# Differential output gates in the gate stage, four merge gates raw beside the attention, weight sums in two wide blocks, decay transposes later

## The chip, the core and the metric

The kernel runs on one core of one Trainium2 chip. TensorE (PE in the rows) multiplies, VectorE (DVE), ScalarE (ACT) and GpSimd (POOL) work elementwise, SyncE (SP) and ScalarE issue the transfers. The metric is the device time of one execution in microseconds. All inputs are float32, a batch of one, 1024 tokens, width 1024.

## What is computed

Two layers of a decoder trunk. Each reads one wide projection of the normalised input three ways (forgetting attention, "f"; differential attention, "d"; a gated short convolution), and merges the three branches with sigmoid gates:

```python
def _layer(x, ...):
    h = _rmsnorm(x, pre_g)
    p = h @ w_in
    (fq, fk, fv, ff, fg, dq, dk, dv, dg, cb, cc, cx, cg, mg) = _split_cols(p)
    log_f = jax.nn.log_sigmoid(ff + b_f)
    y_fox = _fox_attention(fq, fk, fv, log_f) * jax.nn.silu(fg)
    y_diff = _diff_attention(rotary(dq), rotary(dk), dv, lam, lam_init, diff_g) * jax.nn.silu(dg)
    y_conv = cb * _short_conv(cc * cx, conv_w) * jax.nn.silu(cg)
    gates = jax.nn.sigmoid(mg + b_m).reshape(b, s, N_BRANCH, D_MODEL)
    m = gates[:, :, 0] * (y_fox @ w_fox) + gates[:, :, 1] * (y_diff @ w_diff) + gates[:, :, 2] * (y_conv @ w_conv)
    return x + _rmsnorm(m @ w_o, post_g)
```

Inside the forgetting attention the decay c is the running sum of log_f over the tokens.

## The kernel before, in words

**Products in three parts.** Every float32 operand is split into a high part (a cast) and a low part (the operand less the high part). mm3 (lines 353 to 355) multiplies low by high, high by low and high by high. One matmul covers 128 rows, 128 weight columns and 512 tokens.

**Strassen pairs.** Most of the projection runs as pairs of two chunks of 128 columns: emit_pair loads the two weight chunks fa and fb (1024 columns each, two halves u and d) and makes four weight tiles from them, x = fa, y (its halves are the sums t2 and t3), z (its halves are t1 and t4) and b (one half of fb). put makes the high part on ScalarE (line 320) and the low part on GpSimd (line 321); the sums are VectorE subtractions (line 323). A pair is then seven products of 12 matmuls. Tiles for high and low parts have three buffers for the four tiles of a pair, so a tile is made while the pair before is still multiplied. The sums t1, t2 and t3 stand in a pool with two buffers (swaps). Each layer has 20 pairs: six for the convolution's and four for its merge gates, four for the differential q and k, and six for output gates and merge gates (gates_spilled), two ahead of the merge pairs and four between and behind the q and k pairs. The rope of q and k has one multiply per step on GpSimd (line 753), the convolution adds on GpSimd (line 561).

**Forget.** After the pairs, forget makes log_f on VectorE and ScalarE in small steps (lines 679 to 692), stops, and then transposes it on TensorE (line 701) and scans it on VectorE (line 703). Between the two parts the layer steps a projection (qk, "f", 2) four times.

**Attention.** Eight windows follow, four of forgetting heads and four of differential heads. In each window other work is interleaved with the attention's own: PLAN lists it. An entry qk or v is a projection, mg and dg a gate chunk that is computed plainly and stored raw, without its activation (24 matmuls of 512 columns for each of two token halves), y is the product of the attention's output and its output gate, split in two parts (y_prep), and br is one merge of the forgetting branch (merge_br: 24 matmuls of 512 columns). Where a gate was stored raw, y_prep runs a sigmoid on ScalarE (line 1124) and one more multiply on VectorE (line 1121), and merge_br runs a sigmoid of 1024 columns (line 1147). In the attention, line 988 is the exponential of the differential heads, lines 871 and 872 split the transposed probabilities, lines 1029 to 1031 multiply them by v, and lines 1044 and 1045 are the logarithm and exponential by which a head's output is normalised. ScalarE has to load a table (ACT_TABLE_LOAD) when it goes from one group of functions to another.

**Behind the attention** come the merges that PLAN does not name, the eight of the differential branch, and the output projection.

**What sets the order.** Each engine runs its instructions in one order. All engines but SyncE are ordered by a scheduler ahead of time, from the program's order and its own costs; SyncE's instructions stand as written. The pool blocks (41 buffers of 128 x 1024) serves the large intermediate tiles in turn. The kernel's layer function makes the gate pairs from all chunks of mg, fg and dg that PLAN does not name, in that order.

Of the kernel before, what the change touches and what calls it, by code (L numbers as in the profile page):

```python
# [11 lines left out]
F32 = mybir.dt.float32  # L12
# [10 lines left out]
P = 128  # L23
# [25 lines left out]
)  # L49
FILLS = {f for w in PLAN for f in w}  # L50
COST = {"v": 20.8, "qk": 20.8, "dg": 10.4, "mg": 10.4, "load": 0.0, "y": 1.0, "br": 5.2}
# [85 lines left out]
class Trunk:  # L137
# [168 lines left out]
    def emit_pair(self, l, i0, i1):  # L306

        nc = self.nc  # L310
        fa, fb = (self.ws.tile([P, 1056], F32, tag="wraw", name=self.nm("wraw"))[:, :1024] for _ in range(2))
        nc.sync.dma_start(fa, self.io["wt"][l, i0])
        nc.sync.dma_start(fb, self.io["wt"][l, i1])
        u, d = slice(0, 512), slice(512, 1024)

        def new():
            return [self.ws.tile([P, 1056], F32R, tag=t, name=self.nm(t))[:, :1024] for t in ("whi", "wlo")]

        def put(w, o, f):
            nc.scalar.copy(w[0][:, o], f)  # L320
            nc.gpsimd.tensor_tensor(out=w[1][:, o], in0=f, in1=w[0][:, o].bitcast(F32), op=ALU.subtract)  # L321

        sub = lambda o, a, b: nc.vector.tensor_tensor(out=o, in0=a, in1=b, op=ALU.subtract)  # L323
        x = new()
        put(x, slice(0, 1024), fa)
        t1, t2 = self.sw(), self.sw()
        sub(t1, fb[:, u], fa[:, u])
        sub(t2, fb[:, d], t1)
        y = new()
        put(y, u, t2)  # L330
        z = new()
        put(z, u, t1)
        t3 = self.sw()
        sub(t3, fb[:, d], fb[:, u])
        sub(t2, fa[:, d], t2)
        put(y, d, t3)
        put(z, d, t2)
        b = new()
        put(b, u, fb[:, d])
        r = lambda t: t.rearrange("p (k c) -> p k c", c=128)  # L340
        x, y, z, b = [[r(t) for t in o] for o in (x, y, z, b)]
        lo4, hi4 = (lambda p: [t[:, :4] for t in p]), (lambda p: [t[:, 4:] for t in p])
        return dict(b11=lo4(x), b21=hi4(x), t2=lo4(y), t3=hi4(y), t1=lo4(z), t4=hi4(z), b22=lo4(b))
# [867 lines left out]
    def layer(self, l):  # L1211
# [42 lines left out]
        decay = self.forget(L)  # L1254
        next(decay)
        first = self.qk_unit(L, "f", 2)
        for _ in range(4):
            next(first)
        run(decay)
        run(first)  # L1260
# [3 lines left out]
        for n, spec in enumerate(PLAN):  # L1264
# [6 lines left out]
            for f in spec:  # L1271
# [8 lines left out]
                elif f[0] == "load":  # L1280
                    gens.append(self.load_head(L, f[1]))
                    f = ("qk", "d", f[1])
# [136 lines left out]
```

## Time and profile before

| | us |
|---|---|
| median of three runs (2508.68 to 2515.22) | 2514.5 |
| profiled execution | 2515.5 |
| its span in the trace | 2513.7 |
| TensorE busy | 2406.0 (96%) |
| VectorE busy | 1539.6 (61%) |
| ScalarE busy | 1120.4 (45%) |
| GpSimd busy | 865.3 (34%) |

Layer 0 runs from 0 to about 1290 us, layer 1 from there to the end. In layer 0 the pairs run to about 560, the attention from 594 to 1107, the merges to 1175. The profiled execution is 1.8 us longer than its span and lies within the runs shown. In the views, a wait is idle time of an engine, put down to the instruction that released it.

### The profile page before, as it was taken

How to read it: one execution, taken by the hardware profiler on the slowest of the kernel's cores; microseconds unless marked ns; L12 is line 12 of the kernel's file. 1: busy time of each engine (PE TensorE's matmuls, PEld its weight loads, DVE VectorE, ACT ScalarE, POOL GpSimd, SP SyncE). 2: the span in 40 equal slices, each digit the busy share in tenths (PEclk: the TensorE clock that was granted, in tenths of full speed). 3: DMA queues.
4: the chain of work that ended last, by engine and by line, in shares of the span. 5: the costliest groups of instructions: out<-in, count | busy, mean ns of one | idle time of the engine just before them, and what ended most of it. 6: DMA issues, size and time to landing. Idle time of an engine off the chain costs nothing. (4 is left out here: it accounts for less than half of the span.)

```text
span 2513.7 us, 35377 instructions
## 1 busy us (share of the span) xinstructions
PE 2406.0 (96%) x12984; PEld 2037.3 (81%) x12984; DVE 1539.6 (61%) x2785; ACT 1120.4 (45%) x2294; POOL 865.3 (34%) x693
## 2 busy tenths in 40 slices
PE   6899999999999999989989999999999999999898
PEld 5677887787899888768967778887889898887688
DVE  4866466645665666667477664356465656667654
ACT  4323334335555545564453232233355655445542
POOL 0657325442222202451026663254322221125500
PEclk9999999999999999999999999999999999999999
DMA  4112234441223333644431122344422233346434
GB/s 162 42 51 72 98 99 140 155 164 53 77 70 118 110 101 114 198 154 151 151 142 43 51 92 84 105 136 146 151 64 74 75 94 108 105 139 212 148 110 184
DMA packets 117948, 285.54 MB, mean 114 GB/s; under 512 B 15616, under 2 KB 36480, under 8 KB 117776
## 3 DMA queue, kind: packets, MB, share of 16 engines
q1 hardware_dynamic: 67568, 212.69, 25.0%
q10 hardware_dynamic: 50208, 70.60, 9.1%
q8 instruction: 103, 1.69, 0.3%
q14 instruction: 69, 0.57, 0.1%
HBM read 196.06 MB, written 68.29 MB: 105 GB/s over the span
## 5 line engine op out<-in xcount | busy, mean ns | idle before, releaser
L281 POOL TENSOR_TENSOR wlo<-wraw,whi 128x1024 fp32r<-128x1024 f32 (+2 forms) x93 | 196.3, 2113 | 609.4 <-ACT whi L278 542.2
L353 PE MATMUL F<-ht,wlo 128*128 128x512 f32 x792 | 329.1, 416 | 0.0
L355 PE MATMUL F<-ht,whi 128*128 128x512 f32 x792 | 314.5, 397 | 0.0
L354 PE MATMUL F<-ht,whi 128*128 128x512 f32 x792 | 314.0, 396 | 0.2 <-DVE ht L375 0.2
L321 POOL TENSOR_TENSOR wlo<-sw,whi 128x512 fp32r<-128x512 f32 x160 | 226.2, 1424 | 218.9 <-ACT whi L320 193.2
L321 POOL TENSOR_TENSOR wlo<-wraw,whi 128x1024 fp32r<-128x1024 f32 x80 | 158.3, 1981 | 174.1 <-ACT whi L320 165.0
L320 ACT CAST whi<-sw 128x512 fp32r<-128x512 f32 x160 | 96.3, 619 | 245.6 <-DVE sw L323 97.3
L988 ACT ACTIVATE p<-S,sm 128x512 f32<-128x512 f32 (+2 forms) x192 | 110.5, 579 | 152.4 <-DVE sm L984 60.2
L355 PEld LDWEIGHTS F<-ht,whi 128*128 128x128 f32 x792 | 149.7, 189 | 33.3
L872 DVE TENSOR_TENSOR pt<-T,pt 128x512 fp32r<-128x512 f32 (+1 forms) x240 | 148.4, 633 | 42.1 <-ACT pt L871 40.1
L937 POOL TENSOR_TENSOR cB<-cB,tri 128x128 f32<-128x128 f32 x128 | 58.5, 462 | 328.6 <-DVE sm L898 276.8
L354 PEld LDWEIGHTS F<-ht,whi 128*128 128x128 f32 x792 | 150.9, 191 | 25.0 <-DVE ht L375 0.9
L353 PEld LDWEIGHTS F<-ht,wlo 128*128 128x128 f32 x792 | 150.6, 190 | 25.1 <-ACT ht L374 0.4
L278 ACT CAST whi<-wraw 128x1024 fp32r<-128x1024 f32 (+2 forms) x126 | 117.8, 940 | 84.1 <-PE F L355 22.5
L871 ACT CAST pt<-T 128x512 fp32r<-128x512 f32 (+1 forms) x240 | 124.4, 544 | 47.2 <-PE T L176 35.6
L833 PE MATMUL S<-qk,qk 128*128 128x512 f32 (+2 forms) x384 | 136.9, 357 | 5.3 <-ACT p L988 5.1
L982 DVE TENSOR_REDUCE sm<-S 128x1 f32<-128x512 f32 (+2 forms) x192 | 102.4, 552 | 54.4 <-PE S L837 27.8
L176 PE MATMUL T<-ident,p 128*128 128x128 f32 x864 | 127.6, 274 | 6.2 <-DVE p L999 4.7
L320 ACT CAST whi<-wraw 128x1024 fp32r<-128x1024 f32 x80 | 66.7, 834 | 140.8 <-PE S L355 43.8
L834 PE MATMUL S<-qk,sw 128*128 128x512 f32 (+2 forms) x384 | 129.3, 343 | 0.0
L905 ACT ACTIVATE p<-p,sm 128x1024 f32<-128x1024 f32 (+7 forms) x128 | 99.6, 779 | 50.8 <-DVE sm L898 38.9
L353 PE MATMUL F<-whi,ht 128*128 128x256 f32 (+1 forms) x416 | 121.0, 291 | 0.0
(379 smaller groups left out, 7060.2 us busy)
## 6 DMA issues: line engine op xcount, KB each, us to landing
wraw<-wt SPq DMA_DIRECT2D x128, 512.0 KB
mg<-tmp ACTq DMA_DIRECT2D x64, 256.0 KB
sw<-qk ACTq DMA_DIRECT2D x256, 64.0 KB
g<-mg SPq DMA_DIRECT2D x32, 512.0 KB
wraw<-wo SPq DMA_DIRECT2D x32, 512.0 KB
x<-x SPq DMA_DIRECT2D x24, 512.0 KB
wraw<-wbr SPq DMA_DIRECT2D x48, 256.0 KB
m<-tmp ACTq DMA_DIRECT2D x32, 256.0 KB
```

The source lines that it names most:

```text
L176: self.nc.tensor.transpose(out, x, self.ident)
L278: nc.scalar.copy(hi, raw)
L281: getattr(nc, eng).tensor_tensor(out=lo, in0=raw, in1=hi.bitcast(F32), op=ALU.subtract)
L320: nc.scalar.copy(w[0][:, o], f)
L321: nc.gpsimd.tensor_tensor(out=w[1][:, o], in0=f, in1=w[0][:, o].bitcast(F32), op=ALU.subtract)
L353: nc.tensor.matmul(ps, wl, xh, start=start and i == 0, stop=False)
L354: nc.tensor.matmul(ps, wh, xl, start=False, stop=False)
L355: nc.tensor.matmul(ps, wh, xh, start=False, stop=stop and i == n - 1)
L833: nc.tensor.matmul(ps[:, :wp], q[:, i * P:(i + 1) * P], k[:, c0:c0 + wp], start=True, stop=False)
L834: nc.tensor.matmul(ps[:, :wp], qsw[:, (i % 2) * P:(i % 2) * P + P], k[:, c0:c0 + wp], start=False, stop=not (last and guard))
L871: self.clock.later(0.1, lambda: nc.scalar.copy(hi, T[:, n0:]))
L872: done = self.clock.later(0.6, lambda: nc.vector.tensor_tensor(out=lo, in0=T[:, n0:], in1=hi.bitcast(F32), op=ALU.subtract))
```

## The change

PLAN no longer names the differential output gates dg 0 to 3; it names the merge gates mg 4 to 7 in the same windows, raw. So the gate pairs of a layer, until now mg 0 to 7 and fg 0 to 3, become mg 0 to 3, fg 0 to 3 and dg 0 to 3: six as before. The y steps of the differential heads then read finished gates, and merges 4 to 7 of the forgetting branch read raw ones. Merge 4 leaves the last window and runs behind the attention. In emit_pair the sums t1 to t3 leave the two swap buffers; two whole blocks sy and sz take all four sums, and y and z are cast and subtracted once each over 1024 columns. The projection in front of the decay's second part is stepped seven times in place of four.

```diff
@@ -42,10 +42,10 @@
     (("qk", "f", 0), ("v", "f", 0)),
     (("qk", "f", 1),),
     (("mg", 8), ("load", 0), ("v", "d", 0), ("mg", 9)),
-    (("mg", 10), ("load", 1), ("mg", 11), ("dg", 0)),
+    (("mg", 10), ("load", 1), ("mg", 11), ("mg", 4)),
     (("mg", 12), ("load", 2), ("v", "d", 1), ("mg", 13)),
-    (("mg", 14), ("load", 3), ("mg", 15), ("y", "f", 0), ("dg", 2), ("y", "f", 1), ("dg", 1), ("y", "f", 2), ("y", "f", 3)),
-    (("dg", 3), ("br", 0), ("br", 1), ("y", "d", 0), ("br", 2), ("y", "d", 1), ("br", 3), ("br", 4), ("y", "d", 2)),
+    (("mg", 14), ("load", 3), ("mg", 15), ("y", "f", 0), ("mg", 5), ("y", "f", 1), ("mg", 6), ("y", "f", 2), ("y", "f", 3)),
+    (("mg", 7), ("br", 0), ("br", 1), ("y", "d", 0), ("br", 2), ("y", "d", 1), ("br", 3), ("y", "d", 2)),
 )
@@ -321,20 +321,15 @@
         sub = lambda o, a, b: nc.vector.tensor_tensor(out=o, in0=a, in1=b, op=ALU.subtract)
-        x = new()
+        x, y, z = new(), new(), new()
         put(x, slice(0, 1024), fa)
-        t1, t2 = self.sw(), self.sw()
-        sub(t1, fb[:, u], fa[:, u])
-        sub(t2, fb[:, d], t1)
-        y = new()
-        put(y, u, t2)
-        z = new()
-        put(z, u, t1)
-        t3 = self.sw()
-        sub(t3, fb[:, d], fb[:, u])
-        sub(t2, fa[:, d], t2)
-        put(y, d, t3)
-        put(z, d, t2)
+        sy, sz = (self.blk([P, 1024], F32, "st") for _ in range(2))
+        sub(sz[:, u], fb[:, u], fa[:, u])
+        sub(sy[:, u], fb[:, d], sz[:, u])
+        sub(sy[:, d], fb[:, d], fb[:, u])
+        sub(sz[:, d], fa[:, d], sy[:, u])
+        put(y, slice(0, 1024), sy)
+        put(z, slice(0, 1024), sz)
         b = new()
         put(b, u, fb[:, d])
@@ -1254,7 +1249,7 @@
         first = self.qk_unit(L, "f", 2)
-        for _ in range(4):
+        for _ in range(7):
             next(first)
         run(decay)
```

Lines behind emit_pair move up by five. Three places in the engines' orders, each before and after.

GpSimd, at the first pair with a rope step, in layer 0. wlo is a low part, wraw a loaded weight, sw and st sums, tmp a q or k tile; before:

```order
L321 TENSOR_TENSOR wlo_2519<-wraw_2492,whi_2518 128x512
L753 TENSOR_TENSOR tmp_2786<-tmp_2786,rope_2717 128x512
L321 TENSOR_TENSOR wlo_2728<-wraw_2723,whi_2727 128x1024
L321 TENSOR_TENSOR wlo_2736<-sw_2732,whi_2735 128x512
L321 TENSOR_TENSOR wlo_2740<-sw_2731,whi_2739 128x512
L321 TENSOR_TENSOR wlo_2740<-sw_2732,whi_2739 128x512
L753 TENSOR_TENSOR tmp_2851<-tmp_2851,rope_2718 128x512
L321 TENSOR_TENSOR wlo_2736<-sw_2743,whi_2735 128x512
L321 TENSOR_TENSOR wlo_2751<-wraw_2724,whi_2750 128x512
```

and after:

```order
L321 TENSOR_TENSOR wlo_2454<-wraw_2432,whi_2453 128x512
L748 TENSOR_TENSOR tmp_2716<-tmp_2716,rope_2652 128x512
L321 TENSOR_TENSOR wlo_2663<-wraw_2658,whi_2662 128x1024
L321 TENSOR_TENSOR wlo_2665<-st_2670,whi_2664 128x1024
L321 TENSOR_TENSOR wlo_2667<-st_2671,whi_2666 128x1024
L748 TENSOR_TENSOR tmp_2781<-tmp_2781,rope_2653 128x512
L321 TENSOR_TENSOR wlo_2681<-wraw_2659,whi_2680 128x512
```

The second half of y (wlo_2736 from sw_2743) stood behind both halves of z and the rope step; now y is whole ahead of z, and the rope step stands behind z.

TensorE, at the decay of layer 0. F is the projection that stands around it, S takes the transposes (L701 before, L696 after); before:

```order
L355 MATMUL F_4278<-ht_107,whi_3958 128x512
L353 MATMUL F_4278<-ht_107,wlo_3959 128x512
L701 MATMUL S_4265<-ident,tmp_4206 8x128 x4
L701 MATMUL S_4271<-ident,tmp_4206 8x128 x4
L354 MATMUL F_4278<-ht_108,whi_3958 128x512
L355 MATMUL F_4278<-ht_107,whi_3958 128x512
```

and after:

```order
L348 MATMUL F_4178<-ht_107,wlo_3875 128x512
L349 MATMUL F_4178<-ht_108,whi_3874 128x512
L350 MATMUL F_4178<-ht_107,whi_3874 128x512
L348 MATMUL F_4178<-ht_110,wlo_3875 128x512
L349 MATMUL F_4178<-ht_111,whi_3874 128x512
L350 MATMUL F_4178<-ht_110,whi_3874 128x512
L348 MATMUL F_4178<-ht_113,wlo_3875 128x512
L349 MATMUL F_4178<-ht_114,whi_3874 128x512
L350 MATMUL F_4178<-ht_113,whi_3874 128x512
L696 MATMUL S_4204<-ident,tmp_4122 8x128 x4
L696 MATMUL S_4210<-ident,tmp_4122 8x128 x4
```

Before, four matmuls of that F bank's projection stood ahead of the transposes; now 18 do, 14 more (the rows show nine of the 18).

ScalarE, at the end of layer 0's last window. O is an attention output, od its copy, g a gate; before:

```order
L1040 ACTIVATE tmp_10118<-O_9945 128x256
L1041 COPY od_9645<-O_9945 128x256
L871 CAST pt_10120<-T_10121 128x384
L1044 ACT_TABLE_LOAD
L1044 ACTIVATE tmp_10118<-O_9945,eps 128x256
L1045 ACT_TABLE_LOAD
L1045 ACTIVATE tmp_10118<-tmp_10118 128x256
L1040 ACTIVATE tmp_10137<-O_10119 128x256
L1041 COPY od_9645<-O_10119 128x256
L1044 ACT_TABLE_LOAD
L1044 ACTIVATE tmp_10137<-O_10119,eps 128x256
L1045 ACT_TABLE_LOAD
```

and after:

```order
L1035 ACTIVATE tmp_9980<-O_9842 128x256
L1036 COPY od_9555<-O_9842 128x256
L866 CAST pt_9982<-T_9983 128x384
L1121 CAST yd_9935<-od_8031 128x512
L1039 ACTIVATE tmp_9980<-O_9842,eps 128x256
L1040 ACTIVATE tmp_9980<-tmp_9980 128x256
L1035 ACTIVATE tmp_10001<-O_9981 128x256
L1036 COPY od_9555<-O_9981 128x256
L1039 ACTIVATE tmp_10001<-O_9981,eps 128x256
```

Of eleven table loads at the end of each layer's attention one is left, ahead of the first sigmoid of the merges behind it.

## Rows read from the trace of the kernel before

**Rows 1.** TensorE's waits, whole program: engine, tile, line, releaser: us, times, longest

```profile
PE S L353 <- POOL wlo L321: 14.1, 4, 8.2
...
PE F L353 <- POOL wlo L321: 9.8, 3, 3.7
...
PE S L701 <- DVE tmp L692: 5.8, 2, 2.9
```

**Rows 2.** Stretches: length, busy time and instructions of each engine, granted clock, DMA share, GB/s

```profile
95.20:105.50 10.30, 5.52 (x13) 4.35 (x14) 9.97 (x10) 1.62 (x3) 4.87 (x4) 0.50 0.15 51
...
573.10:576.50 3.40, 3.40 (x9) 2.64 (x8) 3.25 (x4) 0.59 (x1) 0.00 (x0) 0.50 0.00 0
...
1467.40:1474.20 6.80, 5.96 (x14) 4.71 (x15) 3.01 (x5) 2.58 (x4) 4.32 (x3) 0.50 0.10 39
```

**Rows 3.** Groups by form: line, engine, tile, shape, count, busy us, mean ns, idle before

```profile
L321 POOL TENSOR_TENSOR wlo<-sw,whi 128x512 fp32r<-128x512 f32 x160 | 226.2, 1424 | 218.9 <-ACT whi L320 193.2 <-DVE tmp L527 25.6
...
L321 POOL TENSOR_TENSOR wlo<-wraw,whi 128x1024 fp32r<-128x1024 f32 x40 | 98.2, 2454 | 130.3 <-ACT whi L320 130.3
...
L320 ACT CAST whi<-sw 128x512 fp32r<-128x512 f32 x160 | 96.3, 619 | 245.6 <-DVE sw L323 97.3 <-PE S L355 44.9 <-PE T L355 28.2
...
L320 ACT CAST whi<-wraw 128x1024 fp32r<-128x1024 f32 x40 | 42.0, 1049 | 117.1 <-PE S L355 35.8 <-issue 22.7 <-PE F L355 21.1
```

**Rows 4.** Timeline of a pair that keeps pace: start, us, instruction, idle before, releaser

```profile
150.82 1.28 POOL L321 TENSOR_TENSOR wlo<-sw,whi 128x512 fp32r<-128x512 f32 x1 [2.73 <-ACT whi L320]
...
153.66 2.54 POOL L321 TENSOR_TENSOR wlo<-sw,whi 128x512 fp32r<-128x512 f32 x2 [1.56 <-ACT whi L320]
...
154.98 1.76 DVE L323 TENSOR_TENSOR sw<-wraw 128x512 f32<-128x512 f32 x1 [1.39 <-POOL wlo L321]
...
156.67 0.68 DVE L323 TENSOR_TENSOR sw<-wraw,wraw 128x512 f32<-128x512 f32 x1
...
157.48 1.29 POOL L321 TENSOR_TENSOR wlo<-sw,whi 128x512 fp32r<-128x512 f32 x1 [1.28 <-ACT whi L320]
...
158.25 0.40 PE L353 MATMUL S<-s,wlo 128*128 128x512 f32 x1
...
161.06 0.40 PE L353 MATMUL T<-s,wlo 128*128 128x512 f32 x1
```

**Rows 5.** Timeline of the pair of the rope step shown above

```profile
479.97 1.29 POOL L321 TENSOR_TENSOR wlo<-sw,whi 128x512 fp32r<-128x512 f32 x1 [3.79 <-ACT whi L320]
...
483.09 0.40 PE L353 MATMUL O<-s,wlo 128*128 128x512 f32 x1
...
485.25 1.72 POOL L753 TENSOR_TENSOR tmp<-tmp,rope 128x512 f32<-128x512 f32 x1
...
488.69 0.50 PE L353 MATMUL F<-s,wlo 128*128 128x512 f32 x1 [2.67 <-POOL wlo L321]
```

**Rows 6.** Timeline of the first pair of layer 0, and GpSimd behind it

```profile
99.98 0.79 PE L353 MATMUL S<-s,wlo 128*128 128x512 f32 x1 [8.18 <-POOL wlo L321]
...
104.56 1.28 POOL L561 TENSOR_TENSOR cv<-cv,tmp 128x512 f32<-128x512 f32 x1 [2.42 <-DVE tmp L527]
```

**Rows 7.** Timeline of TensorE at the decay transposes of layer 0

```profile
571.80 1.04 PE L701 MATMUL S<-ident,tmp 128*8 128x128 f32 x8 [2.88 <-DVE tmp L692]
```

**Rows 8.** TensorE's waits, whole program: products of probabilities and v

```profile
PE O L1030 <- DVE pt L872: 4.1, 2, 3.2
PE O L1029 <- ACT pt L871: 3.2, 2, 1.6
...
PE O L1029 <- ACT tmp L1044: 2.0, 2, 1.1
```

**Rows 9.** Timeline of ScalarE and TensorE at the end of layer 0's last window

```profile
1092.34 1.28 ACT L1124 ACT_TABLE_LOAD   x1
...
1093.64 0.63 ACT L1124 ACTIVATE g<-g 128x512 f32<-128x512 f32 x1
1094.17 0.46 ACT L871 CAST pt<-T 128x384 fp32r<-128x384 f32 x1
...
1095.62 0.58 PE L1030 MATMUL O<-pt,vd 128*128 128x256 f32 x1 [3.16 <-DVE pt L872]
```

## The prediction

> **What bounds the kernel now.** I read the profile in five steps. First the busy shares: TensorE is busy 96% of the span, so time can only come from its waits and from stretches in which it runs at half its clock; VectorE (61%), ScalarE (45%) and GpSimd (34%) matter only where TensorE waits for them. Second the list of TensorE's waits over the whole program [rows 1]: the largest sums that the change can touch are S and F products (L353) waiting for GpSimd's low parts (L321), 14.1 and 9.8 us, and the decay transposes (L701) waiting for VectorE, 5.8 us. Third the stretches behind those waits [rows 2]: TensorE's granted clock is 0.5 to 0.51 there, the 1.2 GHz level in place of 2.4, so a wait costs more than its length. Half of the busy time in such a stretch is loss. Fourth the timelines at a pair that keeps pace, at one that doesn't and at the first one [rows 4 to 6]. Fifth the end of the attention [rows 8, 9].
>
> **Weight sums.** A Strassen pair needs x, y, z and b in high and low parts. Before, y and z are made in halves: casts of 619 ns and lows of 1424 ns, beside 1049 and 2454 ns for 1024 columns [rows 3]. Work falls little: two casts fewer, and two wide lows (4.9 us) for four halves (5.7 us) per pair. What changes is order. The sums share two swap slots, so the third sum (y.d) can be made only when a low has given its slot back; in [rows 4] the sub at 154.98 follows the low y.u, and the low of y.d, behind z.u and z.d, runs 157.48 to 158.77. The fourth product needs it; it starts at 161.06, 12 matmuls after the third at 158.25, so one takes (161.06 - 158.25) / 12 = 0.23 us (0.232 over longer runs). So a pair that keeps pace has 2.3 us to spare, and anything put on GpSimd ahead of y.d makes TensorE wait. [rows 5] show it: the rope multiply (1.72 us) runs ahead of y.d and the product starts 2.67 us late. With the sums in two blocks no sub waits for GpSimd, and y is complete, in one low, before z and b.
>
> What replaces it: y must be whole before the third product, which so far needs only y.u. Cast and low get longer by 1049 - 619 and 2454 - 1424 ns, 1.5 us. In [rows 4] y.u ended at 152.10; whole it ends at 153.6, 4.6 us ahead of the third product. At the rope pair [rows 5] y.u ended at 481.26, whole at 482.8, and the product starts at 483.09: 0.3 us to spare. That holds, if barely. The block slots that the sums take are given back early enough in the order that I read; the lookahead does not change.
>
> The first pair of layer 0 gets a new wait. GpSimd's order now has the convolution multiply-add (L561) ahead of the next pair's x. It waits for a VectorE product and ran at 104.56 to 105.84 [rows 6]; x would follow, 2.45 us, until 108.3. TensorE without its 8.2 us wait [rows 1] is through the fourth to seventh product 4 x 12 x 0.23 = 11.1 us after 91.8 (the wait began at 99.98 less 8.18 [rows 6]), at 102.9. So up to 5.4 us of that wait come back; VectorE reaches the product perhaps a little earlier, since it no longer stalls on a slot in between. I take 4 us and 2 us of half clock.
>
> Sum: 14.1 + 9.8 = 23.9 us of waits; half clock behind four of them, half of 5.52 and of 5.96 us [rows 2], and two more stretches (at 224.9 and 1344.5) as long as the one of 3.40 us that stands for them, together 9.1 us; less 6 at the first pair: **27 us**. Ends: 35 (nothing comes back, and smaller waits of the same kind go too) and 12 (half goes).
>
> **Decay transposes.** In layer 0 TensorE stands 2.88 us at L701 [rows 7], in layer 1 as long (5.8 over two). The wait began at 571.80 - 2.88 = 568.9. In the new order 14 more matmuls of the same projection stand ahead of the transposes, 14 x 0.232 = 3.2 us, so TensorE arrives at 568.9 + 3.2 = 572.1, and the operand is there at 571.8. The margin is 0.3 us. The decay's output is first used in the attention, from 594 on, so nothing behind it comes late. Gain 5.8, and half of the 3.40 us at half clock behind it in layer 0 [rows 2], 1.7: **7.5 us**, between 5 and 8.
>
> **Gates and the end of the attention.** The number of gate pairs is the same before and after, so TensorE's work there is, too. Eight more VectorE multiplies per layer (0.68 us of this shape alone, the sub at 156.67 [rows 4]) and a scratch tile lie beside 7 x 12 x 0.232 = 19.5 us of matmuls per pair: nothing. If they are in the way of a sum it is 0.7 us out of 4.6. In the merge behind the attention four more sigmoids of 1024 columns per layer (about 1.05 us, by the cast of that width [rows 3]) lie beside 24 matmuls (5.6 us) each: nothing.
>
> At the attention's end y of the differential heads no longer needs a sigmoid. That takes away eight activations and eight multiplies per layer, and with them table loads: one takes 1.28 us [rows 9], and the new order has one load in place of eleven there, 10 x 1.28 = 12.8 us per layer out of ScalarE's queue, in which the casts (pt, L871) and the tail of the normalisation (L1044) stand that attention waits for. In [rows 9] the load at 1092.34 stands ahead of the cast at 1094.17, behind which TensorE waits 3.16 us. Over both layers these waits are 4.1 + 3.2 + 2.0 = 9.3 us [rows 8]. Against it: merge 4 leaves the last window, 24 x 0.232 = 5.6 us per layer of matmuls that had covered waits there; they run after the attention instead, so nothing is saved on them. ScalarE is lighter by 12.8 + 8 x 0.63 = 17.8 us per layer, three times the cover that goes, so I let the waits go: **9 us**. Ends: 20 (other waits of that window and half clock behind them go too) and -11 (no wait goes and the cover's 11.1 us stands open).
>
> Here a rule of the Trainium skill speaks. The trace first: the activation at 1093.64 starts 0.02 us after its load has ended [rows 9]. The Trainium skill, ScalarE: Activation LUTs, What ACT_TABLE_LOAD costs, adds a drain of about 1.38 us to each load of 1.28, 2.66 in all. By it ScalarE would come free by 10 x 2.66 = 27 us per layer and the gain would lie at its upper end, 2461; the rows show no such drain.
>
> **Sum.** 27 + 7.5 + 9 = 43.5 us off the profiled execution of 2515.5 us: 2472. The median of the runs shown lies 1.0 us below that execution, so I forecast 2471.
>
> **Rivals.**
> - *The last window is starved.* Its length is set by VectorE and the softmax chain and not by ScalarE's loads. Then no wait goes and merge 4 adds 5.6 us per layer: 2471 + 20 = 2491. For it: VectorE is as busy as ScalarE there; against it: the largest wait stands right behind a load.
> - *Half of the sums' waits come back*, at the first pairs and at the rope pairs with 0.3 us to spare: 27 becomes 13, 2485.
> - *The change does not free the sums:* whole y and z are late as often as y.d was. Then 27 becomes 0: 2498. Against it is the slack of 4.6 us.
> - *Slower, by the shared access of VectorE and GpSimd.* A sub beside a low of GpSimd takes 1.76 us, alone 0.68 [rows 4]; it ended 0.54 us after the two lows had. If a sub has to stand until the low beside it ends, a wide low holds it up to 2.4 us where a half held it 1.3. Where the four subs meet x's wide low, y is late by 2.4 - 0.3 = 2.1 us at each of the eight pairs that have a rope step, with half clock behind it, 1.7: 8 x 3.8 = 30 us, and no gain elsewhere in the sums. That gives 2498 + 30 = 2528. It decides as soon as a sub at these pairs is held more than 0.3 us. The order speaks against it: the subs now wait for nothing but the weights and run early. The rule of the page: the Trainium skill, SBUF — State Buffer, Who interferes with whom, says that a VectorE instruction with two SBUF inputs and a GpSimd instruction that reads SBUF exclude each other for the whole instruction; the 1.76 us agree with it.
>
> **How the numbers follow.** Forecast 0.60 (2455 to 2483), starved window 0.14, half of the sums 0.14, sums not freed 0.05, slower by shared access 0.05, no change for another reason 0.02. The range takes the upper ends (35 + 7.5 + 20 = 62 off: 2452) and reaches past the starved window to 2496; that leaves out some 0.15. About 0.3% (7.5 us) is what a measurement of this kernel tells from no change: faster 0.88, same 0.06, slower 0.06.
>
> **What would show it.** Right: no wait at L701; waits of products for L321 under 8 us, most at the first pair of layer 0; one table load per layer at the attention's end, and the three waits there under 3 us in sum. Wrong: products waiting on GpSimd at each rope pair, subs of over 2 us there, or waits in the last window that grow because no merge matmuls are left to put between.

## The result, and the profile after

The changed kernel takes 2486.2 us in the median (2483.4 to 2486.6, four runs) against 2514.9 for the kernel before: a ratio of 0.989, with a 95% interval of 0.987 to 0.990. It is 28.6 us faster, where 43.5 were forecast: inside the range (2452 to 2496), but 3 us above the band of 2455 to 2483 that had the chance of 0.60. A second series gave 2486.4 and 0.989 again. The profiled execution took 2486.4 us, its span 2484.6.

The list of TensorE's waits after the change, where [rows 1, 8] stand for before (line numbers are five lower, L348 is the former L353, L321 keeps its number; columns: us in total, times, longest):

```profile
PE T L176 <- DVE hn L398: 20.3, 5, 11.2
PE T L176 <- ACT ht L410: 11.2, 7, 3.5
PE S L348 <- POOL wlo L321: 10.3, 5, 5.2
...
PE F L348 <- POOL wlo L321: 5.7, 3, 3.2
...
PE O L1025 <- DVE pt L867: 3.2, 4, 0.9
PE O L348 <- POOL wlo L321: 2.5, 2, 1.9
...
PE O L1024 <- ACT pt L866: 0.7, 2, 0.3
```

Three things are to be seen. The row of the decay (5.8 us) is gone. The three rows of the last window, 9.3 us, are down to 3.9. But products still wait 18.5 us for low parts, against 26.4 before (14.1, 9.8, and two rows of 1.3 and 1.2). The 11.2 us in the first row are the start of the program; the list of before has that wait, too (11.5 us), put down to the input's transfer.

To see where the 29.1 us of span went, take the start of the same TensorE instructions in both profiles: the first product that uses a sum, the first matmul of the attention, the first transpose of the next layer's rows; the last stretch ends at the last matmul. Between them TensorE does the same work before and after (merge 4 moves within its stretch):

| us | pairs and decay, layer 0 | attention to output, layer 0 | border of the layers | pairs and decay, layer 1 | attention to output, layer 1 |
|---|---|---|---|---|---|
| before | 505.4 | 648.6 | 95.1 | 496.6 | 671.5 |
| after | 495.9 | 642.9 | 99.0 | 486.6 | 663.8 |
| difference | -9.5 | -5.7 | +3.9 | -10.0 | -7.7 |

Of the 19.5 us of pairs and decay some 7.6 are the decay (e3 below, and its two waits), so the sums brought 12. The end of the attention brought 13.4, and the border between the layers, of which the prediction said nothing, took 3.9 back. TensorE's busy time fell by 6.8 of the 29.1 us (2406.0 to 2399.2), with the granted clock up from 0.988 to 0.991 in the mean; the rest is waits. Single executions differ, too: in e4 below, whose edit does not touch the pairs, their two stretches came out 2.1 us shorter and 1.8 us longer than before.

The timeline of the first pair of layer 0, answering [rows 6] (start, us, instruction, idle before, releaser):

```profile
103.57 0.68 DVE L522 TENSOR_TENSOR tmp<-uv,O 128x512 f32<-128x512 f32 x1
...
104.39 1.27 POOL L556 TENSOR_TENSOR cv<-cv,tmp 128x512 f32<-128x512 f32 x1 [8.01 <-DVE tmp L522]
...
105.62 2.35 POOL L321 TENSOR_TENSOR wlo<-wraw,whi 128x1024 fp32r<-128x1024 f32 x1
...
108.02 0.79 PE L348 MATMUL S<-ht,wlo 128*128 128x512 f32 x1 [5.24 <-POOL wlo L321]
```

This is the new wait that the prediction worked out: GpSimd stands 8 us idle at the convolution's instruction (L556, the former L561: a multiply, not an add), x follows, and TensorE waits 5.24 us (the bound was 5.4, I took 4).

The wait at 229 us was not foreseen. The timeline of the changed kernel there:

```profile
218.23 5.58 POOL L370 TENSOR_TENSOR ycl<-cv,ych 128x1024 fp32r<-128x1024 f32 x2 [2.90 <-ACT ych L369]
218.65 2.90 DVE L323 TENSOR_TENSOR st<-wraw,wraw 128x512 f32<-128x512 f32 x1
...
221.47 2.89 DVE L323 TENSOR_TENSOR st<-wraw 128x512 f32<-128x512 f32 x1
...
223.76 1.74 POOL L321 TENSOR_TENSOR wlo<-wraw,whi 128x512 fp32r<-128x512 f32 x1
...
225.53 0.33 SPq L312 DMA_DIRECT2D wraw<-wt  x1
...
227.89 1.05 ACT L320 CAST whi<-wraw 128x1024 fp32r<-128x1024 f32 x1 [0.47 <-ACT tmp L622]
...
229.01 2.36 POOL L321 TENSOR_TENSOR wlo<-wraw,whi 128x1024 fp32r<-128x1024 f32 x1 [3.51 <-ACT whi L320]
...
231.43 0.51 PE L348 MATMUL O<-ht,wlo 128*128 128x512 f32 x1 [1.93 <-POOL wlo L321]
```

Read it from the top. Two low parts of the convolution's output (L370) take GpSimd 5.58 us; b's low part stands behind them and ends at 225.50; only then is the weight buffer free, and the load of the next x is issued at 225.53. Meanwhile two subtractions on VectorE take 2.9 us each instead of 0.68. So x is late. Before, the sums were what came last; now it is x, at five of the ten places at which products wait (14.1 of the 18.5 us); z comes late at three and b at two.

The subtractions themselves no longer wait for GpSimd but for the weights. The groups by form (count, busy us, mean ns, idle before and releasers), of before and of after:

```profile
L323 DVE TENSOR_TENSOR sw<-wraw,sw 128x512 f32<-128x512 f32 x80 | 77.5, 969 | 70.9 <-POOL wlo L321 69.8
L323 DVE TENSOR_TENSOR sw<-wraw 128x512 f32<-128x512 f32 x40 | 60.6, 1516 | 37.1 <-POOL wlo L321 37.1
```

```profile
L323 DVE TENSOR_TENSOR st<-wraw,st 128x512 f32<-128x512 f32 x80 | 76.4, 955 | 0.6
...
L323 DVE TENSOR_TENSOR st<-wraw,wraw 128x512 f32<-128x512 f32 x40 | 51.5, 1288 | 75.4 <-DMA wraw<-wt 66.3 <-POOL wlo L321 4.9 <-issue 4.1
```

At the border, TensorE after the change:

```profile
1265.20 0.83 PE L176 MATMUL T<-ident,hn 128*128 128x128 f32 x4 [1.69 <-ACT ht L410]
...
1267.03 1.12 PE L176 MATMUL T<-ident,hn 128*128 128x128 f32 x4 [1.00 <-ACT ht L410]
...
1275.58 0.66 PE L176 MATMUL T<-ident,hn 128*128 128x128 f32 x2 [7.44 <-DVE hn L398]
...
1277.69 0.79 PE L348 MATMUL S<-ht,wlo 128*128 128x512 f32 x1 [1.44 <-POOL wlo L281]
```

and before:

```profile
1278.40 0.82 PE L176 MATMUL T<-ident,hn 128*128 128x128 f32 x6
...
1280.91 0.66 PE L176 MATMUL T<-ident,hn 128*128 128x128 f32 x4
...
1282.81 0.60 PE L176 MATMUL T<-ident,hn 128*128 128x128 f32 x4
...
1291.29 0.66 PE L176 MATMUL T<-ident,hn 128*128 128x128 f32 x2 [6.50 <-DVE hn L403]
```

Before, matmuls of the next layer's first projection stood between the groups of transposes and covered them; after, 18 transposes stand in a row, and the projection's second weight chunk is lowered so late (1.44 us) that it couldn't have covered them.

### The profile page after: what moved, and what is told of

Read it like the earlier page. It is cut to its first block, busy times and chain, and to the rows that moved or that the text cites. A ratio compares the mean times of both kernels' runs of the same rounds, so it can differ in the third digit from the quotient of the medians.

```text
span 2484.6 us, 35310 instructions
## 1 busy us (share of the span) xinstructions
PE 2399.2 (97%) x12984; PEld 2032.6 (82%) x12984; DVE 1554.9 (63%) x2785; ACT 1081.6 (44%) x2186; POOL 834.1 (34%) x613
## 5 line engine op out<-in xcount | busy, mean ns | idle before, releaser
L348 PE MATMUL F<-ht,wlo 128*128 128x512 f32 x792 | 328.9, 415 | 6.7 <-POOL wlo L321 5.1
L321 POOL TENSOR_TENSOR wlo<-st,whi 128x1024 fp32r<-128x1024 f32 x80 | 201.5, 2521 | 182.3 <-ACT whi L320 172.9
L321 POOL TENSOR_TENSOR wlo<-wraw,whi 128x1024 fp32r<-128x1024 f32 x80 | 156.2, 1953 | 198.7 <-ACT whi L320 146.3
L348 PEld LDWEIGHTS F<-ht,wlo 128*128 128x128 f32 x792 | 150.5, 190 | 32.7 <-POOL wlo L321 6.2
L349 PEld LDWEIGHTS F<-ht,whi 128*128 128x128 f32 x792 | 150.8, 190 | 23.9
L320 ACT CAST whi<-st 128x1024 fp32r<-128x1024 f32 x80 | 83.7, 1048 | 127.2 <-PE S L350 30.6
L348 PE MATMUL F<-whi,ht 128*128 128x256 f32 (+1 forms) x416 | 121.0, 291 | 0.0
```

Of the source, the lines that this page charges most:

```text
L348: nc.tensor.matmul(ps, wl, xh, start=start and i == 0, stop=False)
L349: nc.tensor.matmul(ps, wh, xl, start=False, stop=False)
```

## The experiments

Medians are of five rounds (three for e4), each against the kernel before on the same chip, whose medians were 2512.6, 2513.5, 2513.7 and 2513.4 in the four series (e1 to e4, e5 to e8, e9 to e11, e12).

**e1: the weight sums alone.** The kernel before with emit_pair of the changed kernel (that hunk of the diff, nothing else; its lines are those of the changed kernel).

> The kernel before with emit_pair alone changed. My theory: of the 26.4 us that products waited for low parts, about 12 to 15 us go with their half clock (2500 to 2503 us): the old waits behind the swap slots vanish, and waits for x take part of their place (about 5 us at the first pair of layer 0, about 2 us each where the wide lows of the convolution output stand ahead). The wait of 3.2 us at the pair behind the first rope pair, seen in the changed kernel, is absent here, because it comes from the gates. Rival: the sums gain the 27 us of the forecast (2488 us), and the gates give it back.

Measured 2504.6 us, 0.9966 (0.9953 to 0.9978): 8 us (a little less than the theory's 2500 to 2503), and 10.4 by the profiles; pairs and decay take 500.0 and 490.6 us, 5.4 and 6.0 less than before. So the sums never had 27 us to give, and nothing that the gates do takes it away. Waits for low parts fall from 26.4 to 17.8 us, where the theory had 12 to 15 us go:

```profile
PE S L348 <- POOL wlo L321: 8.8, 4, 5.2
...
PE O L348 <- POOL wlo L321: 5.0, 4, 1.9
...
PE F L348 <- POOL wlo L321: 4.0, 2, 2.9
```

One point of my theory fell: the wait behind the first rope pair (2.9 us) is here, too, so the gates do not make it.

**e2: the gates alone.** The kernel before with the new PLAN.

> The kernel before with the list of attention fills (PLAN) alone changed, so gates and merge 4 move. My theory: last window and merges gain 12 to 14 us of waits and half clock over both layers, the border between the layers loses about 4 us (18 transposes stand in a row ahead of the matmuls that were between them), a gate's store ahead of a cast may cost 3 us: 2504 to 2508 us. Rival: the border's loss belongs to the weight sums, not to the gates: 2500 to 2502 us here, and no wait of over 7 us at the border.

Measured 2508.6 us, 0.9982 (0.9973 to 0.9991). Attention to output falls by 5.0 and 9.5 us, the border rises from 95.1 to 98.5: both as the theory said, so the border's loss is the gates'. But pairs and decay of layer 1 take 502.7 us, 6.1 more than before. The old weight sums wait longer when the gates alone move, 30.7 us in all; the largest step, from 3.7 to 5.9 us, is at the first pair behind the border, at 1344 us:

```profile
PE S L353 <- POOL wlo L321: 20.4, 6, 8.2
...
PE F L353 <- POOL wlo L321: 6.9, 3, 3.4
...
PE O L353 <- POOL wlo L321: 3.4, 1, 3.4
```

**e3: the decay alone.**

```diff
         first = self.qk_unit(L, "f", 2)
-        for _ in range(4):
+        for _ in range(7):
             next(first)
```

> The kernel before with the projection stepped seven times ahead of the decay transposes, nothing else. My theory: the two waits at the transposes (2.9 us each) and the half clock behind the first go, 7 to 8 us: 2507 us. Rival: the scan behind the transposes makes the next evacuation late, and 3 us or less are gained.

Measured 2507.2 us, 0.9976 (0.9966 to 0.9986), 5.3 us by the medians and 8.1 by the profiled executions' spans; pairs and decay fall by 4.9 and 2.7 us, 7.6 together, and no wait of TensorE at the transposes is left. The theory holds.

**e4: the table loads.** The kernel before with the gate's sigmoid in y_prep replaced by a copy.

```diff
-                later(4.0, lambda g1=g1: nc.scalar.activation(g1, g1, AF.Sigmoid))
+                later(4.0, lambda g1=g1: nc.scalar.activation(g1, g1, AF.Copy))
```

> The kernel before with the sigmoid of the differential heads' gates replaced by a copy of the same shape (so that the gate's nonlinearity is left out). ScalarE then has as many activations and VectorE as many multiplies, but the ten table loads per layer at the attention's end go. My theory: the loads are what TensorE waited for in the last window; the three waits there (9.3 us over both layers) fall under 3 us, 2502 to 2508 us in all. Rival: the multiplies and sigmoids matter, not the loads: 2512 to 2515 us.

Measured 2499.6 us, 0.9947 (0.9932 to 0.9962), 13 us, more than expected. Activations and multiplies are all there; only the loads went. Attention to output takes 642.7 and 663.1 us, what the changed kernel takes (642.9 and 663.8). The rows of L1030 and L1029 are gone from the list, and the one that comes next in the chain has grown:

```profile
PE T L176 <- DVE p L999: 9.4, 8, 2.0
```

The table loads are the whole gain of that stretch; the multiplies and sigmoids gave nothing that can be seen.

**e5: the changed kernel again**, beside the next three.

> The changed kernel as it is, beside the next three. My theory: 2486 us, 26 to 28 us under the kernel before; more than the 17 us that the medians of the three parts alone sum to, since the gates alone make the old weight sums wait longer (their profile has 7 us more loss in the pairs than the kernel before). Rival: the parts add up, 2493 to 2496 us, and the rest was noise.

Measured 2486.4 us, 0.9890 (0.9876 to 0.9903). The medians of the parts alone add up to 17.3 us (8.0, 4.0, 5.3), their profiles to 23.9 (10.4, 5.4, 8.1); together they gave 27.1 here and 29.1 by the profiles. There is a surplus, but its size depends on which is asked.

**e6: blocks without width.** The changed kernel with y and z in halves:

```diff
-        put(y, slice(0, 1024), sy)
-        put(z, slice(0, 1024), sz)
+        for w, s in ((y, sy), (z, sz)):
+            for o in (u, d):
+                put(w, o, s[:, o])
```

> The changed kernel with y and z cast and lowered in halves out of the two blocks (order y.u, y.d, z.u, z.d), so blocks without wide instructions. If the blocks bring the gain of the sums and width nothing: within 3 us of the changed kernel. If a wide low matters because it holds VectorE for its whole length (2.9 us for a subtraction or a rope add that alone takes 0.7): faster by 3 to 6 us, VectorE's longest two-operand instructions fall from 2.9 to 1.8 us. If four more instructions per pair matter on GpSimd: slower by 3 to 6 us.

Measured 2479.5 us, 0.9864 (0.9850 to 0.9877), 7 us under the changed kernel, where 3 to 6 were expected. (Its lines behind 338, and those of e9 and e12, are one higher than in the changed kernel.) So blocks without width are better than the change as it was made. VectorE's subtractions are held less: over all forms they take 154.5 us in place of 168.4, and those over 2.5 us fall from eleven to four; I had expected none over 1.8. The form shown took 1288 ns with wide lows:

```profile
L323 DVE TENSOR_TENSOR st<-wraw,wraw 128x512 f32<-128x512 f32 x40 | 36.5, 912 | 80.7 <-DMA wraw<-wt 76.4 <-issue 4.2
```

Products wait 14.3 us for low parts, against 18.5: the waits at 199, 229, 1353 and 1463 us are gone, and two of 2.2 us stand for b at 203 and 1433, behind the convolution's low parts. How much of the 7 us is VectorE's and how much is y.u being ready earlier was not separated.

**e7: the convolution's multiplies off GpSimd.** The changed kernel with

```diff
-                eng = nc.vector if x is None else nc.gpsimd
+                eng = nc.vector
```

> The changed kernel with the convolution's multiplies (L556) on VectorE in place of GpSimd. My theory: they hold up the low parts behind them on GpSimd; the wait of 5.2 us at the first pair of layer 0 falls to 2 us or less, those at 199, 1353 and 1433 us (1.3 us each) go: 2477 to 2481 us against 2486. Rival: x comes late there because VectorE is late, and more work on VectorE makes it later: 2486 to 2490 us.

Measured 2472.8 us, 0.9838 (0.9824 to 0.9851), 13.6 us under the changed kernel, more than I expected; waits for low parts fall by 7.0 of it (18.5 to 11.5), and the rest was not traced. The wait at the first pair is gone, with those at 199, 1353 and 1433:

```profile
PE F L348 <- POOL wlo L321: 6.3, 2, 3.5
...
PE O L348 <- POOL wlo L321: 3.2, 2, 2.8
PE T L348 <- POOL wlo L321: 1.5, 2, 0.7
PE S L348 <- POOL wlo L321: 0.6, 1, 0.6
```

The rival, that VectorE's own lateness holds x there, falls: VectorE has more to do and x is on time. The waits behind the convolution's low parts grew, from 1.9 to 2.8 us.

**e8: its low parts too.** e7 with

```diff
-            self.split(hi, lo, t, self.nc.gpsimd)
+            self.split(hi, lo, t)
```

> The one before with the low parts of the convolution's output (L370, 1024 columns, 2.7 us on GpSimd) on VectorE too. My theory: the waits for x at 229 and 1463 us (2.1 us each, with half clock) go, because b's low part gives the weight buffer back earlier: 3 to 6 us under the one before. Rival: VectorE, on which the sums stand, gets the queue instead, and the waits stay: within 2 us of it.

Measured 2467.8 us, 0.9816 (0.9802 to 0.9829), 5 us under e7. The two waits fall from 2.8 us each to 1.0 and 1.3. So GpSimd's queue ahead of b's low part is, for the larger part, what gave the weight buffer back late.

**e9: all three.** e8 with the halves of e6.

> The changed kernel with all three edits of the runs before: convolution multiplies and the low parts of its output on VectorE, y and z in halves out of the blocks. My theory: the gains come from different places (halves: 7 us, GpSimd freed: 19 us) but both shorten the same waits for low parts, of which 6 us are left in the second; so 2462 to 2467 us, a few us under the best so far (2468). Rival: halves put more instructions in VectorE's and GpSimd's way at the convolution: 2468 to 2472 us.

Measured 2462.4 us, 0.9798 (0.9785 to 0.9811). Of the 26.4 us that products waited for low parts in the kernel before, two rows are left, and the larger is the pair behind the first rope pair:

```profile
PE F L349 <- POOL wlo L321: 3.4, 1, 3.4
...
PE S L349 <- POOL wlo L321: 0.3, 1, 0.3
```

**e10: sums and gates, decay as before.** The changed kernel with the loop at four again.

> The changed kernel with the projection stepped four times again ahead of the decay transposes (so weight sums and gates changed, decay as before). My theory: gates and sums belong together, the old sums are what loses 7 us in the pairs when the gates alone move; so this lies 20 us or more under the kernel before (2491 to 2495), against 12 us for the sum of the two parts alone (2501). Rival: the parts add, and the surplus is in the decay step: 2499 to 2502 us.

Measured 2495.6 us, 0.9931 (0.9918 to 0.9943), 18.1 us under the kernel before: between the two answers. By stretches: on top of the gates the new sums take pairs and decay from 506.6 and 502.7 us (e2) to 503.0 and 491.1, 15.2 us, against 11.4 on the kernel before (e1). So sums and gates help each other by about 4 us by the stretches, in layer 1 only, and by 6 by the medians (18.1 against 8.0 and 4.0). The rest of the surplus comes with the decay's step: on top of sums and gates it brings 9.0 us by the medians (27.1 less 18.1), alone 5.3. Two waits for low parts that e10 has at 479 and 495 us (0.4 and 1.5 us) are not in the changed kernel.

**e11: merge 4 kept in the last window**, its gate's sigmoid left out.

```diff
-    (..., ("br", 3), ("y", "d", 2)),
+    (..., ("br", 3), ("br", 4), ("y", "d", 2)),
...
+            if (br, dc) == (0, 4):
+                nc.scalar.activation(g, g, AF.Copy)
+            else:
+                nc.scalar.activation(g, g, AF.Sigmoid, bias=self.par[:, i:i + 1])
```

> The changed kernel with merge 4 kept in the last window, its gate's sigmoid left out (a copy of the same shape in its place, for a sigmoid there brings the table loads back). My theory: merge 4 gives the last window nothing (its waits are not longer without it), and what it changes is the border between the layers, where the transposes are again spread between matmuls: 3 to 5 us under the changed kernel, 2481 to 2483 us. Rival: merge 4 covers waits of the last window: these fall by 4 us or more per layer, and the border stays as it is; or neither: 2486 us.

Measured 2480.0 us, 0.9869 (0.9856 to 0.9883), 6.4 us under the changed kernel, a little more than expected. The border is back at 94.1 us, and attention to output takes 643.2 and 661.8 us, what it takes without merge 4 in the window (642.9 and 663.8). So the window is not starved by merge 4's going, and its place alone moves the border.

**e12: a version of its own.** e9 with merge 4 in the last window; dg 3, whose y is made behind the attention, is stored raw in its place and mg 4 goes to the gate stage.

```diff
-    (("mg", 10), ("load", 1), ("mg", 11), ("mg", 4)),
+    (("mg", 10), ("load", 1), ("mg", 11), ("dg", 3)),
...
-    (..., ("br", 3), ("y", "d", 2)),
+    (..., ("br", 3), ("br", 4), ("y", "d", 2)),
```

> The best kernel so far with merge 4 in the last window again, all computed: gate dg 3 is the one stored raw in the fifth window (its y is made behind the attention, so no table load comes into the window) and mg 4 goes to the gate stage. My theory: merge 4's place sets the border between the layers, and 4 to 5 us of waits there go: 2456 to 2459 us against 2462.4. Rival: the border's 4.7 us were tied to the weight sums in wide form, or the window starves again: 2461 us or more.

Measured 2452.7 us, 0.9762 (0.9749 to 0.9775), more than expected: 61 us under the kernel before and 34 under the changed one. The border takes 94.3 us against 98.9 in e9. It is the fastest kernel of the study. The waits for low parts that are left in it, with one of 0.3 us:

```profile
PE F L349 <- POOL wlo L321: 2.9, 1, 2.9
...
PE T L349 <- POOL wlo L321: 1.5, 1, 1.5
```

## Why the prediction came out as it did

**Bound and direction: right.** TensorE is busy 97% after; all that moved are its waits and the half clock behind them.

**Decay: right in mechanism and size.** 7.5 forecast, 7.6 by the stretches of e3 (5.3 by its medians, inside the 5 to 8). TensorE has no wait left at the transposes, with the 0.3 us of margin.

**End of the attention: right in mechanism, somewhat undersized.** 9 us forecast, 13.4 measured, and e4 shows that it is the table loads. The three waits were to fall under 3 us and fell to 3.9; two of 0.8 us for a merge's multiply (L1148) are new. What I had not counted is that the merges' own waits for the low parts of their weights go, too: 6.6 us in the kernel before, none in the changed one's merges and none in e4:

```profile
PE F L353 <- POOL wlo L281: 2.7, 2, 1.6
...
PE T L353 <- POOL wlo L281: 2.2, 2, 1.6
...
PE S L353 <- POOL wlo L281: 1.7, 1, 1.7
```

What I had set against the gain, merge 4's cover, cost nothing (e11), and the rival of the starved window with it. That a load costs ScalarE only its 1.28 us stands: 20 loads fewer gave 13 us, about half of 20 x 1.28 = 25.7, probably as the rest of ScalarE's queue there is off the path. By the prediction's other rule, with a drain, the gain was to be 20 us (2460 by its own terms, not 2461); it was 13.4.

**Weight sums: the step that was mis-sized.** 27 us forecast, 12 measured. The old waits went as told: y no longer comes last, and the pair with the rope step [rows 5] has no wait. The step that failed is the subtraction "less 6 at the first pair". I looked for new waits in the order of GpSimd at one place and took the slack of 4.6 us for y as proof for the rest. But x, not y, is what mostly comes late afterwards: behind the convolution's multiplies (e7), behind its low parts (e8), and once behind the first rope pair. At the first pair itself 5.24 us came back, as reckoned; the nine other places have 13.3, which the sum has nothing for. 18.5 us of waits are left where I allowed 8. The rival that half of the sums' waits come back, 13 us, is in size what happened; its place was half right, at the first pairs, not at the rope pairs. That the whole came out within 2 us of its 2485 is partly luck: the end of the attention gave 4.4 us more than forecast, and the border took 3.9 back.

**The slower rival: its mechanism is there, its price is not.** VectorE's two-operand instructions are held for a whole wide low; the changed kernel has this pair:

```profile
388.88 2.40 POOL L321 TENSOR_TENSOR wlo<-wraw,whi 128x1024 fp32r<-128x1024 f32 x1
388.96 2.87 DVE L750 TENSOR_TENSOR tmp<-tmp,tmp 128x512 f32<-128x512 f32 x1 [0.59 <-POOL tmp L748]
```

The second ends 0.55 us after the first, about its own length. That is what the Trainium skill, SBUF — State Buffer, Who interferes with whom, states: the two exclude each other for the whole instruction. But the subs run early enough that y is not late at the rope pairs. What price there is lies within the 7 us by which halves are faster than wide instructions (e6); how much of them was not separated.

**The border: not in the prediction.** I read the engines' orders at the places where the diff speaks, not at the border, some 150 us behind the merge that moved. It cost 3.9 us.

**Gate stage and merges: nothing, as told.** No wait of TensorE in the gate stage or behind the attention names the new multiplies or sigmoids. That the new list of fills makes the old sums wait longer (e2) was not foreseen. Half of that, some 2.2 of 4.4 us, is at the pair behind the border, where no gate stands: two low parts take GpSimd 4.47 us beside the convolution's work on VectorE, 3.44 before. A gate's multiply can matter, though: in e10 the cast of x at 491.57 us stands on ScalarE behind the store of a dg gate that waits for its multiply (L626), and the product waits 1.5 us.

**Left open.** The wait behind the first rope pair (2.9 to 3.5 us in every kernel with the new sums, in layer 0 only): x's cast stands on ScalarE behind a gate's sigmoid, which waits for VectorE, late after the rope step, and behind the gate's store, which waits for VectorE again. Ahead of that sigmoid stands a table load, and only in layer 0:

```profile
408.32 1.28 ACT L625 ACT_TABLE_LOAD   x1 [0.61 <-DVE tmp L522]
...
411.42 1.04 ACT L320 CAST whi<-wraw 128x1024 fp32r<-128x1024 f32 x1 [1.18 <-DVE tmp L626]
```

Layer 1 has neither load nor wait there, so the load's 1.28 us are likely part of the 3.2. All this is argued from the timeline; no kernel tried it. Nor was it tried whether the 4 us that sums and gates give each other come from the border's new order alone.

## What to carry to other kernels

When a change takes away what comes last at a wait, read the order once more for what comes last then, at every place where the wait stood: here the slack of one tile was checked and the next tile in the queue took half of the gain back. Be wary of making an instruction on GpSimd longer where VectorE has two-operand work beside it: halves were 7 us faster here. Try giving VectorE the work of GpSimd's queue where TensorE waits for that queue, even if VectorE is the busier engine: here that brought 18.6 us, with VectorE 63% and GpSimd 34% busy. And compare the whole order of the engine that bounds the kernel, not only the places that the diff names: one merge of 24 matmuls, moved out of a window, rearranged the border some 150 us later.

## What the runs showed of the hardware

A subtraction of 128x512 on VectorE takes 0.68 us alone, 1.76 beside lows of 512 columns on GpSimd [rows 4] and 2.9 beside lows of 1024: it ends about its own length after GpSimd's instruction. I had counted that as a rare case; in the changed kernel this form of subtraction takes 1288 ns in the mean. A sigmoid in the middle of exponentials and logarithms costs more than its own table load: per layer, two such switches brought ten loads of 1.28 us (four and six), their own, one each for the heads' exponential (L988), and one at each logarithm (L1044) and exponential (L1045) behind them. Without them (e4, and the changed kernel) no load stands between the exponentials and logarithms there; the eleventh, for a sigmoid behind the last of them, is left.
